# Late convolution taps of a hybrid diffusion step: squares in buffers of their own, one PSUM bank per late accumulator and mean, some taps of chunk 0 as diagonal matrix products

## The chip, the cores and the metric

The kernel runs on one core of a Trainium2 chip. The core has a matrix engine (TensorE, PE in the profile), three engines for element-wise work (VectorE or DVE, ScalarE or ACT, GpSimd or POOL) and a queue that issues the DMAs (SyncE, SP). Each engine executes its own list of instructions in order and waits on semaphores for the others. The metric is the device time of one execution in microseconds, lower is better.

## The reference, cut to what matters

The whole reference is one step of a two-layer backbone on 1024 noisy tokens and 128 context tokens, width 1024, all in float32. Layer 0 mixes with a Conformer convolution, layer 1 with attention, and each layer ends with a convolutional FFN. The change lies in the Conformer convolution of layer 0:

```
def dwconv(x, w, b):                      # depthwise, 31 taps, SAME, per channel
    C = x.shape[-1]
    y = lax.conv_general_dilated(x, w[:, None, :].astype(x.dtype), window_strides=(1,), padding='SAME',
                                 dimension_numbers=('NWC', 'WIO', 'NWC'), feature_group_count=C)
    return y + b

def conformer_conv(h, w_pw1, dw_w, dw_b, ln_g, ln_b, w_pw2):
    a, g = jnp.split(h @ w_pw1, 2, axis=-1)
    u = a * jax.nn.sigmoid(g)
    u = dwconv(u, dw_w, dw_b)
    u = jax.nn.silu(layernorm(u, ln_g, ln_b))
    return u @ w_pw2
...
        x = x + g1 * y                    # y: the mixer's output, g1 from silu(cond) @ ada_w + ada_b
        h = modulate(rmsnorm(x, norm2_g[i]), sh2, sc2)
        x = x + g2 * conv_ffn(h, ffn_w_up[i], ffn_conv_w[i], ffn_conv_b[i], ffn_w_down[i])
```

The layer norm is over all 1024 channels of a token.

## The kernel before, in words

Channels lie on the 128 partitions, in eight blocks j = 0 to 7 (KT = 8); the 1152 tokens lie in the free dimension, in three chunks c of 384 (CH, NCH). Each float32 product is made of three products of split operands (`mm3`, lines 245 to 249: high by high, high by low, low by high); small sums such as the mean are plain float32 products.

The convolution stage runs so. `gated` (line 582) makes u for a block j and a chunk c from two projections. For j = 0 to 5 (WHOLE = 6) the 31 taps run over the whole row of 1167 columns: POOL's share (`taps_pool`, line 645) is a multiplication on ACT into a tile of tag `tmp` (two buffers) and an addition on POOL into `pacc`; DVE's share (`taps_vector`, line 656) is a multiply-add into `da`, a PSUM tile of three banks (tag `acc`); `join` (line 666) adds both into U. For j = 6 and 7 the taps are done later and chunk by chunk in `late_taps(c)` (line 699), 15 taps on POOL (POOL_TAPS_LATE) and 16 on DVE. Its accumulators are the first two banks of one three-bank PSUM tile, `late` (line 696), and the mean of the layer norm is written to the third (line 710).

The loop at lines 761 to 769 then does for each chunk: some steps of `later`, `late_taps(c)`, `layer_norm(c)` at high priority, the reload of the residual stream X[c] from DRAM (`reload`, line 386), and `project_residual` (line 747), the projection with w_pw2 (tiles `pw2p`), eight products of 24 matmuls with the residual addition (L384) and the square sum for the next norm (`add_stat`, line 310: a square on ACT, an addition on POOL, L316 and L317). `norm_mod` of the chunk for the FFN is put into `bg` and moves on at the `tick`s of the next projection; in the last one's case in the FFN.

`layer_norm` (line 709): mean by eight float32 products with a constant matrix (L712), subtraction on DVE (L717), squares on ACT (L724), sums of squares on DVE for blocks 0 to 3 and on POOL for 4 to 7 (L727, L730), two small products (`token_rstd`, `spread`), multiplication on DVE (L736), SiLU on ACT (L740), and the split into ln_h on ACT (L743) and ln_l on DVE (L744). The squares take tiles of tag `tmp`, and so do those of `add_stat` in this projection (the last argument of line 768).

`later` (line 580) are the products of the conditioning vector with ada_w (`ada`, line 252; tile `adaw`, three buffers of 512 KB here, loaded by SP), cut into steps; LATER = (8, 0, 6) of them stand ahead of the three chunks, others in `gated` and `project_residual`. The weights of the projections come through a ring of three raw buffers (`w_raw`), each split by ACT (L220) and DVE (L221).

The order of the instructions on SP is that of the program. On the other engines a planner orders them at build time: an instruction goes where its operands are expected, by the planner's costs, to be ready, in order of priority, which is the order of the program save under `tc.high_priority()`. Buffers of a tag are handed out in the order of the program; a new tile waits until the tile that had the buffer has been read for the last time.

The PSUM has eight banks. In this stage `pool.open` gives four to tag `mm`, three to `acc`, one to `ms` (line 482); `norm_mod` and `ada` take `ms`.

Of the kernel before, what the change touches and what calls it, by code (L numbers as in the profile page):

```python
# [8 lines left out]
F32 = mybir.dt.float32  # L9
F32R = mybir.dt.float32r  # L10
AF = mybir.ActivationFunctionType
ALU = mybir.AluOpType
AX = mybir.AxisListType
PSUM = bass.MemoryType.PSUM
DRAM = bass.MemoryType.DRAM

P = 128
D = 1024
KT = D // P
# [3 lines left out]
CH = 384  # L23
# [7 lines left out]
TAPS = 31  # L31
# [6 lines left out]
RING = 3  # L38
SPLITS = 1
PROMPT_LAG = 2  # L40
POOL_TAPS_LATE = 15
WHOLE = 6
LATER = (8, 0, 6)
NORM_POOL = (1, 3, 5, 7)
# [19 lines left out]
def raw32(t):  # L64
    return t.bitcast(F32)
# [14 lines left out]
def tile_hybrid_step(ctx: ExitStack, tc: tile.TileContext, a: dict, outs: list):  # L80
    nc = tc.nc
# [4 lines left out]
    hp = ctx.enter_context(tc.tile_pool(name="hp", bufs=NCH))  # L86
# [25 lines left out]
    def ntile(name, n=CH, dt=F32):  # L112
        return np_.tile([P, n], dt, tag="n", name=name)
# [7 lines left out]
    def htiles(name):  # L121
        hh = hp.tile([P, KT, CH], F32R, tag="hh", name=f"{name}_h")
        hl = hp.tile([P, KT, CH], F32R, tag="hl", name=f"{name}_l")
        return hh, hl

    class Banks:


        stack = None

        def open(self, **slots):
            if self.stack:
                self.stack.close()
            self.stack = ExitStack()
            self.slots = {
                tag: (self.stack.enter_context(tc.tile_pool(name=f"p_{tag}", bufs=b, space=PSUM, reuse_waits="tile")), n)
                for tag, (b, n) in slots.items()
            }

        def __call__(self, tag, name):  # L140
            pool_, n = self.slots[tag]
# [2 lines left out]
    pool = Banks()  # L144
# [13 lines left out]
    ident = cp.tile([P, P], F32, name="ident")  # L158
# [320 lines left out]
            yield from g  # L479


    pool.open(mm=(4, 512), acc=(1, 1536), ms=(1, 512))


    vec_rows = [
# [24 lines left out]
    slot = lambda tag, *args, **kw: (slot_0 if tag in ("adaw", "vrow") else slot_a)(tag, *args, **kw)  # L510
# [22 lines left out]
    X = [xtile(f"x0_{c}") for c in range(NCH)]  # L533
    acc = acc_tile("acc0")
# [44 lines left out]
    us = []  # L579
    later = chain(*(ada(pool, l, g) for l, g in ((0, 1), (0, 2), (1, 0), (1, 1), (1, 2))))  # L580
# [56 lines left out]
    slot = lambda tag, *args, **kw: (slot_a if tag == "u" else slot_c)(tag, *args, **kw)  # L637

    U = [xtile(f"u_{c}") for c in range(NCH)]
    SPAN = [(0, CH), (CH, 2 * CH), (2 * CH, CONV_N)]  # L640

    def tap(j, t):
        return dww[:, j, t : t + 1]
# [12 lines left out]
    def taps_vector(j, u, d, n, s0_, s1_, fresh):  # L656

        for t in range(n):
            src = u[:, s0_ + t : s1_ + t]
            if t == 0 and fresh:  # L660
                nc.vector.tensor_scalar(d, src, tap(j, t), None, ALU.mult)
            else:
                nc.vector.scalar_tensor_tensor(d, src, tap(j, t), d, ALU.mult, ALU.add)
            yield
# [10 lines left out]
    for j in range(KT):  # L675
# [8 lines left out]
        u = us[j][2]  # L684
        da = pool("acc", f"da{j}")
        pacc = slot("pacc", f"pacc{j}")
        t0 = TAPS - POOL_TAPS
# [5 lines left out]

    L = [None] * NCH
    half = KT // 2
    late = pool("acc", "late").rearrange("p (b n) -> p b n", n=512)
    paccs = {j: slot("pacc", f"pacc{j}") for j in range(WHOLE, KT)}

    def late_taps(c):
        s0_, s1_ = SPAN[c]  # L700
        t0 = TAPS - POOL_TAPS_LATE
        for j in range(WHOLE, KT):
            u, d = us[j][2], late[:, j - WHOLE, 0 : s1_ - s0_]
            taps_pool(j, u, paccs[j], t0, s0_, s1_)
            for _ in taps_vector(j, u, d, t0, s0_, s1_, True):
                pass
            join(j, d, paccs[j], c, s0_)

    def layer_norm(c):
        mu = late[:, KT - WHOLE, 0:CH]  # L710
        for j in range(KT):
            nc.tensor.matmul(mu, mean_w, U[c][:, j, :], start=(j == 0), stop=(j == KT - 1))  # L712
        hh, hl = htiles(f"ln{c}")
        ss = [None, None]
        for g in range(2):
            jj = slice(g * half, (g + 1) * half)
            nc.vector.tensor_tensor(  # L717
                U[c][:, jj, :], U[c][:, jj, :], mu.unsqueeze(1).to_broadcast([P, half, CH]), ALU.subtract
            )
            eng = (nc.vector, nc.gpsimd)[g]  # L720
            for i in range(half // 2):
                sq = slot("tmp", f"lnsq{c}_{g}_{i}")[:, 0 : 2 * CH]
                j0 = g * half + 2 * i
                nc.scalar.activation(sq.rearrange("p (j t) -> p j t", t=CH), U[c][:, j0 : j0 + 2, :], AF.Square)  # L724
                if i == 0:
                    ss[g] = ntile(f"lnss{c}_{g}")
                    eng.tensor_tensor(ss[g], sq[:, 0:CH], sq[:, CH:], ALU.add)  # L727
                else:
                    for o in (0, CH):
                        eng.tensor_tensor(ss[g], ss[g], sq[:, o : o + CH], ALU.add)  # L730
        bank = pool("mm", f"lnv{c}")
        rs = token_rstd(pool, ss, f"lnv{c}", bank)
        pb = spread(pool, rs, f"lnv{c}", bank)
        for g in range(2):
            jj = slice(g * half, (g + 1) * half)
            nc.vector.tensor_tensor(  # L736
                U[c][:, jj, :], U[c][:, jj, :], pb.unsqueeze(1).to_broadcast([P, half, CH]), ALU.mult
            )
            for j in range(g * half, (g + 1) * half):
                nc.scalar.activation(  # L740
                    U[c][:, j, :], U[c][:, j, :], AF.Silu, scale=col("conv_ln_g", j), bias=col("conv_ln_b", j)
                )
            nc.scalar.activation(hh[:, jj, :], U[c][:, jj, :], AF.Copy)  # L743
            nc.vector.tensor_tensor(hl[:, jj, :], U[c][:, jj, :], raw32(hh)[:, jj, :], ALU.subtract)  # L744
        L[c] = (hh, hl)

    def project_residual(H, X, c, acc, l, name, tag):
        for m in range(KT):
            w = weights.take()
            ps = project(pool, w, H[c], f"{name}p{c}_{m}")  # L750
            with tc.high_priority():
                residual(ps, X, m, c, l, 2)
                add_stat(acc, m, c, X[c][:, m, :], tag=tag)
            tick()
            if l == 0 and m % 2:
                next(later, None)

    X = [None] * NCH
    H = [None] * NCH
    acc1 = acc_tile("acc1")  # L760
    for c in range(NCH):
        for _ in range(LATER[c]):
            next(later, None)
        late_taps(c)
        with tc.high_priority():
            layer_norm(c)
        X[c] = reload(0, c, "x1_")
        project_residual(L, X, c, acc1, 0, "pw2", "tmp")
        bg.append(norm_mod(pool, X, acc1, c, 0, 1, H, "n1"))

    for _ in later:
        pass
    pool.open(mm=(5, 512), t=(2, 512), ms=(1, 512))
    sC.close()
    sA.close()
    sF, slot = phase(s=(6, NT), g=(4, NT + 3))
# [13 lines left out]
    sK, slot = phase(s=(4 * NKV, SLOT))  # L790
# [128 lines left out]
    for b in QKV_ORDER:  # L919
        ws = [weights.take(), weights.take()]  # L920
        for tt in range(NTT):
            c, t = divmod(tt, CH // P)
            if H[c] is None:
                drain()
            hh, hl = H[c]
# [187 lines left out]
    for s in range(-3, len(steps)):  # L1113
# [4 lines left out]
        if s >= 0:  # L1118
            i, t = steps[s]
# [24 lines left out]
        if s >= 0:  # L1144
            probs.pop(s)
            i, t = steps[s]
# [13 lines left out]
    sF, slot = phase(s=(6, NT), g=(4, NT + 3))  # L1160
    X = [None] * NCH
# [93 lines left out]
```

## Time and profile before

| | us |
|---|---|
| time of the kernel, median of 3 runs (lowest, highest) | 2887.58 (2884.42, 2888.75) |
| the profiled execution | 2887.7 |
| its span, first to last instruction | 2885.8 |
| PE busy | 2692.8 (93%) |
| DVE busy | 1608.9 (56%) |
| ACT busy | 1083.1 (38%) |
| POOL busy | 758.8 (26%) |
| mean granted TensorE clock, share of full | 0.965 |

Busy shares are means over stages with different limits. The page shows PE's busy share in 40 slices of 72 us: the fifth to the eighth (289 to 577 us), which hold the late taps, layer norms and two of the projections, read 4 5 6 4 tenths, where nearly all later slices read 9. In the rows below, a time at the head of a row is in us from the span's start, `x` counts instructions, and square brackets hold the idle time ahead of an instruction and what ended it.

### The profile page before, as it was taken

What the parts mean: (1) busy time and instruction counts of PE and PEld (TensorE: products, weight loads), DVE (VectorE), ACT (ScalarE), POOL (GpSimd) and SP (SyncE); (2) the same over time, 40 slices, a digit from 0 to 9 for tenths busy, and PEclk for the clock granted to TensorE, in tenths of its full rate; (3) what the DMA queues carried; (4) which work ended last, traced back from release to release, by engine and by line L of the source; (5) the groups of instructions that cost most, each with busy time, mean ns of one, the idle gap of its engine ahead of it and who ended that gap; (6) DMA issues with size and microseconds to landing.
All of it is one profiled execution on the core that took longest, in us unless ns stands there. A gap on an engine that the chain in (4) does not pass through costs nothing.

```text
span 2885.8 us, 40019 instructions
## 1 busy us (share of the span) xinstructions
PE 2692.8 (93%) x15863; PEld 2568.6 (89%) x15863; DVE 1608.9 (56%) x2793; ACT 1083.1 (38%) x2110; POOL 758.8 (26%) x840
## 2 busy tenths in 40 slices
PE   7999456499999999999999899999999999999999
PEld 4888155299999999999999889989999999999998
DVE  6899746355444444445464578876544444444445
ACT  5555444342222222221365677765421222122222
POOL 3799643520000000000256556644200000000003
PEclk9999677799999999999999999999999999999999
DMA  7554233331111111111120000025211111111111
GB/s 252 181 156 146 95 110 103 94 104 43 44 45 44 44 45 44 38 43 37 64 93 29 1 1 1 1 79 163 73 37 44 45 44 37 44 44 32 43 52 66
DMA packets 194419, 192.18 MB, mean 67 GB/s; under 512 B 7072, under 2 KB 173323, under 8 KB 192698
## 3 DMA queue, kind: packets, MB, share of 16 engines
q1 hardware_dynamic: 193946, 189.53, 21.0%
q8 instruction: 125, 2.05, 0.3%
q14 instruction: 60, 0.49, 0.1%
q0 software_dynamic: 288, 0.11, 0.0%
HBM read 175.19 MB, written 14.42 MB: 66 GB/s over the span
## 4 chain that ended last, share of the span: by engine, by line
PE 87%; DVE 6%; POOL 3%; DMA 2%; ACT 2%; issue 1%; SPq 0%; DVEq 0%; POOLq 0%; ACTq 0%
PE f1pd L247 3%; PE f1pd L249 3%; PE f1pd L248 3%; PE f1pg L249 3%; PE f0pg L249 3%; PE f1pg L248 3%; PE f0pg L248 3%; PE f0pv L247 3%; PE f1pv L247 3%; PE f0pg L247 3%; PE f1pg L247 3%; PE f1pv L248 3%; PE f0pv L248 3%; PE f0pv L249 3%; PE f1pv L249 3%; PE f0pd L247 3%
## 5 line engine op out<-in xcount | busy, mean ns | idle before, releaser
L220 ACT ACTIVATE w_hi<-w_raw 128x1024 fp32r<-128x1024 f32 x208 | 218.1, 1058 | 923.2 <-PE f0pd L248 223.7
L221 DVE TENSOR_TENSOR w_lo<-w_raw,w_hi 128x1024 fp32r<-128x1024 f32 x208 | 280.6, 1358 | 425.9 <-ACT w_hi L220 425.7
L654 POOL TENSOR_TENSOR pacc<-pacc,tmp 128x1167 f32<-128x1167 f32 (+2 forms) x156 | 291.4, 1870 | 36.1 <-ACT tmp L653 13.5
L384 DVE SCALAR_TENSOR_TENSOR x<-f1pd,mods,x 128x256 f32<-128x256 f32 (+1 forms) x352 | 170.2, 514 | 102.7 <-PE f1pd L249 102.4
L384 DVE SCALAR_TENSOR_TENSOR x<-f0pd,mods,x 128x256 f32<-128x256 f32 (+1 forms) x352 | 169.8, 514 | 99.1 <-PE f0pd L249 98.9
L411 POOL MEMSET f1gp<- 128x1 f32 x66 | 3.6, 99 | 703.8 <-DVE f1gp L435 690.8
L411 POOL MEMSET f0gp<- 128x1 f32 x66 | 3.6, 99 | 703.8 <-DVE f0gp L435 690.8
L1063 POOL TENSOR_TENSOR pr<-pr,sm 128x384 f32<-128x384 f32 x192 | 154.0, 831 | 107.4 <-DVE sm L1061 53.8
L653 ACT ACTIVATE tmp<-u,dww 128x1167 f32<-128x1167 f32 (+2 forms) x156 | 142.6, 918 | 97.0 <-POOL pacc L654 94.6
L248 PE MATMUL f1pd<-f1al,w_hi 128*128 128x384 f32 x528 | 178.6, 338 | 0.0
L249 PE MATMUL f1pd<-f1ah,w_lo 128*128 128x384 f32 x528 | 178.5, 338 | 0.0
L249 PE MATMUL f0pd<-f0ah,w_lo 128*128 128x384 f32 x528 | 178.5, 338 | 0.0
L248 PE MATMUL f0pd<-f0al,w_hi 128*128 128x384 f32 x528 | 178.4, 338 | 0.0
L247 PE MATMUL f1pd<-f1ah,w_hi 128*128 128x384 f32 x528 | 178.4, 339 | 0.0
L247 PE MATMUL f0pd<-f0ah,w_hi 128*128 128x384 f32 x528 | 177.8, 338 | 0.0
L249 PE MATMUL f0pg<-n_h,w_lo 128*128 128x384 f32 x528 | 176.5, 334 | 0.0
L249 PE MATMUL f1pg<-n_h,w_lo 128*128 128x384 f32 x528 | 176.5, 334 | 0.0
L248 PE MATMUL f0pg<-n_l,w_hi 128*128 128x384 f32 x528 | 176.5, 334 | 0.0
L248 PE MATMUL f1pg<-n_l,w_hi 128*128 128x384 f32 x528 | 176.5, 334 | 0.0
L247 PE MATMUL f0pg<-n_h,w_hi 128*128 128x384 f32 x528 | 176.4, 334 | 0.0
L247 PE MATMUL f1pg<-n_h,w_hi 128*128 128x384 f32 x528 | 176.4, 334 | 0.0
L248 PE MATMUL f0pv<-n_l,w_hi 128*128 128x384 f32 x528 | 176.4, 334 | 0.0
(323 smaller groups left out, 7829.5 us busy)
## 6 DMA issues: line engine op xcount, KB each, us to landing
adaw<-in_ada_w_dram SPq DMA_DIRECT2D x96, 512.0 KB, 5.0
w_raw<-in_ffn_w_up_dram SPq DMA_DIRECT2D x88, 512.0 KB, 3.8
w_raw<-in_ffn_w_down_dram SPq DMA_DIRECT2D x44, 512.0 KB, 3.7
w_raw<-in_conv_w_pw_dram SPq DMA_DIRECT2D x40, 512.0 KB, 7.0
w_raw<-in_attn_w_o_dram SPq DMA_DIRECT2D x24, 512.0 KB, 4.3
xs_d<-x SPq DMA_DIRECT2D x6, 1536.0 KB, 11.5
x<-xs_d SPq DMA_DIRECT2D x6, 1536.0 KB, 7.0
w_raw<-in_attn_w_qkv_dram SPq DMA_DIRECT2D x12, 512.0 KB, 3.7
```

The costliest lines, as they stand in the source:

```text
L220: nc.scalar.activation(hi, raw, AF.Copy)
L221: nc.vector.tensor_tensor(lo, raw, raw32(hi), ALU.subtract)
L247: nc.tensor.matmul(ps, wh, mh, start=first, stop=False)
L248: nc.tensor.matmul(ps, wh, ml, start=False, stop=False)
L249: nc.tensor.matmul(ps, wl, mh, start=False, stop=last)
L384: nc.vector.scalar_tensor_tensor(xx, ps[:, lo:hi], mod(l, v, j, cond), xx, ALU.mult, ALU.add)
L411: nc.gpsimd.memset(gp[:, z : z + 1], 0.0)
L653: nc.scalar.activation(tmp, u[:, s0_ + t : s1_ + t], AF.Copy, scale=tap(j, t))
L654: nc.gpsimd.tensor_tensor(d, d, tmp, ALU.add)
L1063: nc.gpsimd.tensor_tensor(pr[n], pr[n], ri.to_broadcast([P, CH]), ALU.mult)
```

## The change

The late taps get a table LATE_TAPS with two numbers a chunk: how many taps are products on PE, and how many are POOL's. Chunk 0 has 12 on PE, 7 on POOL and 12 on DVE; chunks 1 and 2 have none on PE, 12 on POOL and 19 on DVE. A tap on PE is a float32 product of u with a 128x128 diagonal matrix that ACT makes from the identity and the tap's column; twelve of them accumulate in the bank to which DVE adds its taps. The matrices lie in a tile of tag `hh`. The steps of `later` that stood ahead of a chunk's taps stand behind these products now.

The three-bank tag `acc` is closed after the whole blocks and replaced by `la`, three tiles of one bank: each late accumulator and each mean is a tile of its own. The squares of the layer norm lie in one tile of tag `hl`, and the sums go into the first square of each half in place of a tile of their own; the squares of `add_stat` in this projection take tiles of the norm pool (`ntile`, six buffers). So `tmp` serves the taps alone.

```
-POOL_TAPS_LATE = 15
+LATE_TAPS = ((12, 7), (0, 12), (0, 12))
...
-    pool.open(mm=(4, 512), acc=(1, 1536), ms=(1, 512))
+    pool.open(mm=(4, 512), ms=(1, 512))
+    sacc = ExitStack()
+    pool.add(sacc, acc=(1, 1536))
...
-    late = pool("acc", "late").rearrange("p (b n) -> p b n", n=512)
+    sacc.close()
+    pool.add(sacc, la=(3, 512))
...
     def late_taps(c):
         s0_, s1_ = SPAN[c]
-        t0 = TAPS - POOL_TAPS_LATE
-        for j in range(WHOLE, KT):
-            u, d = us[j][2], late[:, j - WHOLE, 0 : s1_ - s0_]
+        n, t0 = LATE_TAPS[c]
+        t0 = TAPS - t0
+        te = t0 - n
+        ds = {j: pool("la", f"late{j}_{c}")[:, 0 : s1_ - s0_] for j in range(WHOLE, KT)}
+        if n:
+            diag = hp.tile([P, (KT - WHOLE) * n, P], F32, tag="hh", name=f"diag{c}")
+            for i, (j, t) in enumerate((j, t) for j in ds for t in range(te, t0)):
+                nc.scalar.activation(diag[:, i, :], ident, AF.Copy, scale=tap(j, t))
+                nc.tensor.matmul(
+                    ds[j], diag[:, i, :], us[j][2][:, s0_ + t : s1_ + t], start=(t == te), stop=(t == t0 - 1)
+                )
+        for _ in range(LATER[c]):
+            next(later, None)
+        for j, d in ds.items():
+            u = us[j][2]
             taps_pool(j, u, paccs[j], t0, s0_, s1_)
-            for _ in taps_vector(j, u, d, t0, s0_, s1_, True):
+            for _ in taps_vector(j, u, d, te, s0_, s1_, not n):
                 pass
             join(j, d, paccs[j], c, s0_)
     def layer_norm(c):
-        mu = late[:, KT - WHOLE, 0:CH]
+        mu = pool("la", f"mu{c}")[:, 0:CH]
...
+        sq = hp.tile([P, KT, CH], F32, tag="hl", name=f"lnsq{c}")
...
-                sq = slot("tmp", f"lnsq{c}_{g}_{i}")[:, 0 : 2 * CH]
                 j0 = g * half + 2 * i
-                nc.scalar.activation(sq.rearrange("p (j t) -> p j t", t=CH), U[c][:, j0 : j0 + 2, :], AF.Square)
...
+                nc.scalar.activation(sq[:, j0 : j0 + 2, :], U[c][:, j0 : j0 + 2, :], AF.Square)
+                ss[g] = sq[:, g * half]
+                for j in range(j0, j0 + 2):
+                    if j > g * half:
+                        eng.tensor_tensor(ss[g], ss[g], sq[:, j], ALU.add)
...
     for c in range(NCH):
-        for _ in range(LATER[c]):
-            next(later, None)
         late_taps(c)
...
-        project_residual(L, X, c, acc1, 0, "pw2", "tmp")
+        project_residual(L, X, c, acc1, 0, "pw2", None)
...
+    sacc.close()
     pool.open(mm=(5, 512), t=(2, 512), ms=(1, 512))
```

`pool.add` is the loop that opens PSUM tags, taken out of `Banks.open` so that a tag can be closed by itself.

## Rows read from the trace of the kernel before

**Rows 1.** Busy us by stretch: PE, PEld, DVE, ACT, POOL; PE clock, DMA share, GB/s.
```profile
311.00:371.00 60.00, 21.17 (x61) 9.89 (x57) 40.92 (x60) 28.54 (x42) 27.72 (x28) 0.61 0.11 36
371.00:411.00 40.00, 37.20 (x205) 34.70 (x205) 16.77 (x18) 13.11 (x18) 9.86 (x7) 0.95 0.67 197
411.00:478.00 67.00, 19.72 (x63) 15.00 (x64) 38.48 (x56) 32.01 (x51) 34.00 (x35) 0.57 0.00 0
478.00:514.00 36.00, 35.67 (x209) 31.21 (x207) 16.09 (x20) 13.95 (x20) 13.54 (x11) 1.00 0.88 263
514.00:587.00 73.00, 31.07 (x99) 17.06 (x100) 29.55 (x43) 32.92 (x53) 35.89 (x35) 0.65 0.20 65
587.00:622.00 35.00, 33.86 (x196) 33.18 (x195) 18.27 (x30) 13.33 (x19) 14.08 (x11) 1.00 0.67 196
```
**Rows 2.** Waits of PE, 311 to 622: us in total, times, longest.
```profile
PE late L712 <- DVE u L669: 62.3, 3, 29.6
PE pw2p L247 <- ACT ln_h L743: 21.9, 3, 8.1
```

**Rows 3.** Timeline of POOL, tap additions of the three chunks: start, us.
```profile
314.27 24.53 POOL L654 TENSOR_TENSOR pacc<-pacc,tmp 128x384 f32<-128x384 f32 x23 [0.72 <-ACT tmp L653]
...
411.52 29.86 POOL L654 TENSOR_TENSOR pacc<-pacc,tmp 128x384 f32<-128x384 f32 x28
...
515.07 15.43 POOL L654 TENSOR_TENSOR pacc<-pacc,tmp 128x399 f32<-128x399 f32 x14
```

**Rows 4.** Timeline of ACT, squares of the first layer norm.
```profile
349.15 1.58 ACT L724 ACTIVATE lnsq<-u 128x768 f32<-128x768 f32 x2 [11.85 <-DVE u L717]
...
353.17 0.84 ACT L724 ACTIVATE lnsq<-u 128x768 f32<-128x768 f32 x1 [1.10 <-POOL lnss L727]
```

**Rows 5.** Timeline of DVE, late taps and joins, and the next norm.
```profile
311.86 9.84 DVE L663 SCALAR_TENSOR_TENSOR late<-u,dww,late 128x384 f32<-128x384 f32 x15
323.92 0.56 DVE L669 TENSOR_TENSOR u<-late,pacc 128x384 f32<-128x384 f32 x1 [2.23 <-POOL pacc L654]
324.51 0.62 DVE L661 TENSOR_SCALAR late<-u,dww 128x384 f32<-128x384 f32 x1
...
353.48 5.22 DVE L663 SCALAR_TENSOR_TENSOR late<-u,dww,late 128x384 f32<-128x384 f32 x8
...
426.50 0.56 DVE L669 TENSOR_TENSOR u<-late,pacc 128x384 f32<-128x384 f32 x1 [15.79 <-POOL pacc L654]
427.09 0.62 DVE L661 TENSOR_SCALAR late<-u,dww 128x384 f32<-128x384 f32 x1
...
467.94 3.23 DVE L356 SCALAR_TENSOR_TENSOR n_u<-x,gsc,n_b 128x384 f32<-128x384 f32 x6
```

**Rows 6.** Busy us of L712 (PE, PEld) by stretch, PE clock, DMA share, GB/s.
```profile
339.40:344.10 4.70, 4.65 (x8) 2.53 (x9) 0.50 0.01 3
344.10:347.30 3.20, 3.17 (x10) 1.62 (x8) 0.97 0.00 0
```

**Rows 7.** Timeline of PE, ada products beside the late taps of chunk 0.
```profile
313.33 4.40 PE L270 MATMUL ada<-adaw,cs 128*32 128x512 f32 x12 [1.34 <-DMA adaw<-in_ada_w_dram]
```

**Rows 8.** Chain of work in time, mean of chunk 0 and start of its projection.
```profile
339.45 7.83 PE late L712 x16
...
371.34 0.69 PE pw2p L248
```

**Rows 9.** Groups by line and shape: busy us, mean ns of one, idle before.
```profile
L859 ACT ACTIVATE qk_1xn<-pqkv,qk_r 128x128 f32<-128x128 f32 x10 | 3.1, 365 | 1.7 <-POOL qk_r L334 1.7
```

**Rows 10.** Timeline of DVE, two weight splits.
```profile
262.70 3.71 DVE L221 TENSOR_TENSOR w_lo<-w_raw,w_hi 128x1024 fp32r<-128x1024 f32 x1
...
388.56 1.22 DVE L221 TENSOR_TENSOR w_lo<-w_raw,w_hi 128x1024 fp32r<-128x1024 f32 x1 [2.46 <-ACT w_hi L220]
```

**Rows 11.** Groups by line and shape on DVE, 311 to 622.
```profile
L744 DVE TENSOR_TENSOR ln_l<-u,ln_h 128x1536 fp32r<-128x1536 f32 x6 | 10.5, 1756 | 5.4 <-ACT ln_h L743 5.4
```

**Rows 12.** Timeline of SP, the ada loads ahead of chunk 2.
```profile
505.10 24.25 SPq L258 DMA_DIRECT2D adaw<-in_ada_w_dram  x10
```

More of the change, by code (lines that the diff above doesn't have):

```diff
@@ L134, in open, with add @@
             self.stack = ExitStack()
[L135 to L138, printed above, removed]
+            self.slots = {}
+            self.add(self.stack, **slots)
+        def add(self, stack, **slots):
+            for tag, (b, n) in slots.items():
+                pool_ = tc.tile_pool(name=f"p_{tag}", bufs=b, space=PSUM, reuse_waits="tile")
+                self.slots[tag] = (stack.enter_context(pool_), n)
         def __call__(self, tag, name):
@@ L721, in layer_norm @@
             for i in range(half // 2):
-                sq = slot("tmp", f"lnsq{c}_{g}_{i}")[:, 0 : 2 * CH]
                 j0 = g * half + 2 * i
-                nc.scalar.activation(sq.rearrange("p (j t) -> p j t", t=CH), U[c][:, j0 : j0 + 2, :], AF.Square)
[L725 to L730, printed above, removed]
+                nc.scalar.activation(sq[:, j0 : j0 + 2, :], U[c][:, j0 : j0 + 2, :], AF.Square)
[3 more added lines that the diff above has]
+                        eng.tensor_tensor(ss[g], ss[g], sq[:, j], ALU.add)
         bank = pool("mm", f"lnv{c}")
```

## The prediction

> **What bounds the kernel now.** I read the busy time by stage first [rows 1]. Three chunks of 384 tokens pass one after the other through an approach (late taps, then the layer norm) and a projection (pw2p). The approaches take 60, 67 and 73 us, with TensorE (PE) busy 21, 20 and 31 us of them at a mean granted clock of 0.57 to 0.65; the projections take 40, 36 and 35 us with PE nearly full. The reader is to see that the approach of a chunk begins only where the projection before it ends: 200 us of approach in a row, between stages that PE fills.
>
> Then PE's waits in that stretch [rows 2]: 62.3 us for the join of the late taps (L669) and 21.9 us for ln_h, the end of the layer norm. So the path runs through taps, join, mean, layer norm, projection, three times.
>
> Then who makes the join late. On POOL [rows 3] the 28 tap additions of chunk 1 run in one piece from 411.52, and chunk 2's from 515.07; in chunk 0's projection POOL is busy 9.9 of 40 us [rows 1]. It could have begun earlier: u and pacc are long there. What holds it is the two tmp buffers. The squares of the layer norm and those of the projection take them as well, in the order of the program, so a tap of chunk 1 gets one only after chunk 0's last square. The squares themselves show it: two leave at 349.15, the fourth at 353.17 waits for a POOL addition to give its buffer back [rows 4]. DVE has the other half of it [rows 5]: j=6 of chunk 1 ran inside the layer norm of chunk 0 (eight taps from 353.48), but the first tap of j=7 stands at 427.09, directly behind the join of j=6 at 426.50, and in chunk 0 likewise (324.51 behind 323.92, although DVE had idled 2.23 us). All late accumulators and the mean are one PSUM tile.
>
> **The change, part by part.** The sum is made against the profiled execution: 2887.7 us, of which the span is 2885.8 and 1.9 lies around it; the median of the runs is 2887.58, the same for this purpose.
>
> *Diagonal products.* For j=6 and j=7 of chunk 0, PE takes 12 taps each: 24 products with a 128x128 fp32 weight over 384 columns. That is the shape of the mean product L712, of which the trace has two passes a product, 16 in all: seven filled 4.65 us at clock 0.50 (the eighth only touches that window), nine 3.17 us at 0.97 [rows 6], 0.66 and 0.35 us a pass. So a product costs 1.33 us at half clock and 0.70 at full, 24 cost between 17 and 32 us. L712 itself ran its first seven passes at half clock, so I take four products at half clock and twenty at full, 19.3 us. They can't start before the accumulator of j=5, whose banks they take, is joined: 311.2, where the first late tap stands now (0.66 before the second at 311.86 [rows 5]). PE also holds the ada products, which wait for their loads at that time (12 in 4.40 us behind a wait of 1.34 [rows 7]); I add 1 us to either twelve. Then j=6's products end at 323 (311.2 + 4 x 1.33 + 8 x 0.70 + 1) and j=7's at 332.5. DVE adds its 12 taps behind each: 12 x 0.656 us (the fifteen of a row in 9.84 [rows 5]) = 7.9, a join 0.6: j=6 joined at 331.5, j=7 at 341. Before, the mean began at 339.45 [rows 8]. This part costs 1.5 us: DVE idles 12 us for the products and saves 8 taps, 5.2 us. Bounds: -3 (all at full clock, no ada in the way) to +19 us (all at half clock, then 12 taps and the join, with 8 us of ada ahead of them). Building 24 diagonals is ACT work on 128x128 with a scale per partition; the nearest row takes 0.365 us [rows 9], so 9 us. They lie between 272 and 311, where ACT only feeds POOL; without that cover they would be late by 9 us, which is inside the bound.
>
> *POOL and ACT.* POOL's additions fall from 28 a chunk to 12, 22 and 22. At 1.07 us (23 in 24.53 [rows 3]) and 1.10 for chunk 2 (14 in 15.43), with 4 of chunk 0's before 311 (28 less the 23 and one shortly ahead), the last of chunk 0 is done at about 321, of chunk 1 at 345, of chunk 2 at 369 plus 4 for the layer norm. Nothing else asks for tmp now. So POOL leaves the path altogether: it is done with the last chunk when the first projection begins. The squares leave in one piece (4 x 0.84 us), which takes 1.4 us from each layer norm. Against that, POOL's additions now run under DVE's work. DVE's w_lo, with both inputs in SBUF, took 3.71 us where POOL ran long tap additions and 1.22 where it was idle [rows 10], while taps, with one input in PSUM, keep 0.656 beside them. Five instructions of the first layer norm have both inputs in SBUF (three sums of squares, two of L744); with at most one 1.0 us addition in front of each they cost up to 5 us; I take 1.4, so that the first layer norm keeps its length.
>
> The Trainium skill, page "SBUF — State Buffer", section "Who interferes with whom", says that a VectorE instruction with two SBUF inputs contends with a GpSimd instruction that reads SBUF, and that the one that comes second waits for the whole of the other. The w_lo pair agrees. It speaks against moving additions under the layer norm; by it the first projection would begin up to 5 us later, less the 1.4 already counted, and the sum end near 2795.
>
> *A bank for each accumulator and mean.* Three banks go round: j=6, j=7, mean. Chunk 1's j=6 may start when chunk 0's j=6 is joined, j=7 when j=7 is, without a wait for the mean or the other join. DVE's taps are now 12, 19, 19 in place of 16 for each j.
>
> *DVE, which becomes the engine to count.* From 341: the mean takes 7.83 us, the rest of the layer norm to the projection 24.1 (371.34 - 347.3) [rows 8]. In these DVE had room for 11 taps (7.8/0.656, idle before) and 16 (as before). Of chunk 1's 38 taps 11 are left when the projection begins at 373 (341 + 31.9; 371.3 before). There DVE is busy 16.8 of 40 us [rows 1]; 11 taps (7.2) and the joins (1.1) take 8.3/0.58 = 14 us: chunk 1 joined at 387. Its mean now meets a PE at full clock: 16 x 0.35 = 5.6, then 24.1: layer norm 1 ready at 417. PE has 40 + 5.6 + 2.4 (mean and small products) of work from 373: the projection ends at 421. So projection 1 starts at 421 in place of 478: 57 us won.
>
> Chunk 2, 38 taps of 399 columns at 0.656 x 399/384 = 0.68: 25.9 us. From 387 to 421 DVE's 34 us go to the projection (11), to layer norm 1 (six of 1.756 as L744 [rows 11], three sums of 0.55: 12.2) and leave 11 us, 16 taps. Left: 22 taps 15.0, joins 1.2, and the norm of chunk 0 for the next stage, which comes first in the program (six of its eight L356 take 3.23 [rows 5], with four L364, taken alike, 6.4): 22.6 us at the 55% that projection 1 leaves (16.1 of 36 busy [rows 1]): 41 us, joined at 462. Mean 5.6, layer norm 24.1: projection 2 at 492, in place of 587: 95 us won. Projection 1 is done on PE at 465 (36 and 8 more), so some 27 us of PE's idleness stay.
>
> *Cover.* The loads: SP issues the ada loads of this stage over 24.25 us from 505.10 [rows 12], 27 us behind the start of projection 1; moved with it they end at 472, before the reload of chunk 2 is free to go at 492. Where that cover is gone each us of lateness goes into projection 2 after four of its products. The squares of add_stat now take buffers of the norm pool; POOL's additions empty them in time, as they did with two.
>
> **Sum.** 2887.7 - 95 = 2793 us. What follows is the same work, held by PE.
>
> **Rivals.**
> (a) Only one chunk hides. DVE is in-order, and if joins and taps of chunk 2 fall behind projection 1 and the norm of chunk 0, chunk 2 stays serial: 57 won, 2831 us. For it: DVE's count above leaves it no slack. Against: the planner did put 16 taps into the gaps of a layer norm [rows 5].
> (b) The change doesn't do what it says: chunk 1's taps still wait for the projection, because another shared thing (ACT's order, the mm banks) holds them. Then only the shorter POOL chains count: chunk 1 goes from 29.9 to 25 us (DVE's 38 taps), chunk 2 by about 8 less, squares 4: 2887.7 - 17 = 2871 us. Against: what stands in front of the additions in [rows 3, 4] is tmp, and the change takes that away.
> (c) Slower, by the diagonal products: PE sits cold behind the ada loads, all 24 cost 1.33 us, and the join of chunk 0 comes 19 us late. It decides if the last of them ends later than 332.5; each us after that is a us on the path. With the taps of the other chunks held as in (b), and half of its 17 us, 2887.7 + 19 - 9 = 2898 us. For it: clock 0.61 in that stretch [rows 1]. Against: it needs the taps of the other chunks to stay in order as well.
>
> **How the numbers follow.** Forecast 0.60, (a) 0.26, (b) 0.08, (c) 0.06. The forecast's own spread is 2768 (projection 0 five us sooner, and chunk 2's taps ahead of the norm, which takes 6.4/0.55 = 12 from its wait, and 8 for a DVE that in all this isn't held up: 120 won) to 2812; (a) spreads to about 2850. Range 2768 to 2845. A measurement tells 0.2%, 5.8 us, from no change. Faster 0.93 (the first two and most of (b)), the same 0.02, slower 0.05.
>
> **What would show it.** POOL's chunk-1 additions start near 321 and not at 411; the first tap of j=7 of chunk 1 stands before the join of its j=6; the mean of chunk 1 lies inside the first projection; PE's wait for L669 falls from 62 to some 35 us; the next stage starts near 527 in place of 622. Wrong: POOL's additions still behind the projection's squares (b), the mean of chunk 0 later than 345 (c), or DVE idle while chunk 2's taps are outstanding (a).

## The result: 2812 us, 0.974 of the kernel before

The changed kernel takes 2812.12 us (median of 4 runs, 2810.35 to 2812.89) against 2888.16 us of the kernel before in runs beside it: a ratio of 0.9738, 95% interval 0.9721 to 0.9755, some 76 us. The profiled execution has a span of 2810.8 us (2885.8 before), mean granted clock 0.981 (0.965).

All of it is won before the FFN. Its first product starts at 544.20 us, before the change at 619.53: 75.3 us earlier, as much as the medians differ by. So the start of the FFN serves below as a second measure beside the ratio. From there to the end the traces below take between 2262.6 and 2268.7 us, so it is good to some 3 us.

The changed kernel by stretch (columns as in [rows 1]; the stretches are the approach of chunk 0, projection 0, the gap behind it, projection 1, the gap behind that, projection 2):

```profile
308.00:382.00 74.00, 39.99 (x127) 20.08 (x125) 55.12 (x92) 42.89 (x68) 55.85 (x55) 0.75 0.14 43
382.00:428.00 46.00, 46.00 (x244) 41.06 (x244) 37.97 (x51) 17.82 (x24) 19.56 (x13) 0.94 0.58 172
428.00:436.40 8.40, 2.73 (x16) 2.16 (x14) 4.89 (x6) 7.28 (x12) 1.86 (x2) 0.72 0.00 0
436.40:488.50 52.10, 46.29 (x230) 41.44 (x230) 27.16 (x34) 20.89 (x32) 17.45 (x14) 0.85 0.61 182
488.50:500.70 12.20, 8.24 (x30) 1.15 (x29) 8.50 (x6) 8.57 (x12) 0.99 (x1) 0.72 0.65 202
500.70:544.20 43.50, 41.82 (x230) 35.82 (x229) 23.70 (x38) 16.77 (x27) 15.42 (x14) 1.00 0.65 196
```

Of the three approaches of 60, 67 and 73 us [rows 1] one is left. Those of chunks 1 and 2 lie inside the stretches before them, and what remains of them are gaps of 8.4 and 12.2 us. The first approach has become longer: projection 0 starts at 381.9, before the change at 369.5.

TensorE's waits from 308 to 545 us (total, times, longest), to be read against [rows 2]:

```profile
PE ada L274 <- DMA adaw<-in_ada_w_dram: 13.0, 7, 3.6
PE pw2p L251 <- ACT ln_h L761: 11.7, 2, 10.8
PE mu L732 <- DVE u L675: 7.7, 1, 7.7
PE mu L732 <- DVE u L738: 4.4, 1, 4.4
PE lnv L346 <- POOL lnv_r L338: 4.2, 1, 4.2
```

The join, 62.3 us in three waits, costs 7.7 us in one. POOL's timeline says why (start, us), against [rows 3]:

```profile
310.61 38.38 POOL L660 TENSOR_TENSOR pacc<-pacc,tmp 128x384 f32<-128x384 f32 x36 [1.53 <-ACT tmp L659]
357.03 1.03 POOL L660 TENSOR_TENSOR pacc<-pacc,tmp 128x399 f32<-128x399 f32 x1 [8.05 <-ACT tmp L659]
...
382.50 5.91 POOL L660 TENSOR_TENSOR pacc<-pacc,tmp 128x399 f32<-128x399 f32 x3 [0.86 <-ACT tmp L659]
```

The 36 additions in one piece, whose row shows only the shape of the first, are the last nine of chunk 0, all 22 of chunk 1 (320.1 to 343.6) and the first five of chunk 2; chunk 1's began at 411.52 before. Chunk 2's are done at 388.4 instead of 551.

DVE's late taps and joins (start, us), against [rows 5]:

```profile
325.72 7.87 DVE L669 SCALAR_TENSOR_TENSOR late<-u,dww,late 128x384 f32<-128x384 f32 x12 [17.71 <-PE late L717]
333.69 0.56 DVE L675 TENSOR_TENSOR u<-late,pacc 128x384 f32<-128x384 f32 x1
...
337.33 12.70 DVE L669 SCALAR_TENSOR_TENSOR late<-u,dww,late 128x384 f32<-128x384 f32 x24 [0.46 <-PE late L717]
349.94 0.55 DVE L675 TENSOR_TENSOR u<-late,pacc 128x384 f32<-128x384 f32 x1
...
417.07 0.62 DVE L675 TENSOR_TENSOR u<-late,pacc 128x256 f32<-128x256 f32 x2
```

DVE stood idle for 17.71 us, waiting for the diagonal products of j=6. Behind them the 12 taps of j=7 of chunk 0 and 12 of chunk 1's j=6 take turns (x24). The last join of chunk 2 ends at 417.7.

On TensorE the products came late, since ada products that waited for their loads stood before them:

```profile
311.04 1.05 PE L274 MATMUL ada<-adaw,cs 128*32 128x512 f32 x4 [1.56 <-DMA adaw<-in_ada_w_dram]
315.04 1.42 PE L274 MATMUL ada<-adaw,cs 128*32 128x512 f32 x4 [2.95 <-DMA adaw<-in_ada_w_dram]
316.39 9.93 PE L717 MATMUL late<-u,diag 128*128 128x384 f32 x26
326.16 4.03 PE L732 MATMUL mu<-u,mean_w 128*128 128x384 f32 x12
330.03 7.26 PE L717 MATMUL late<-u,diag 128*128 128x384 f32 x22
```

### The profile page after: what moved, and what is told of

The parts are those of the page before. It is cut to its first block, busy times and chain, and to the rows that moved or that the text cites. A ratio compares the mean times of both kernels' runs of the same rounds, so it can differ in the third digit from the quotient of the medians.

```text
span 2810.8 us, 40051 instructions
## 1 busy us (share of the span) xinstructions
PE 2697.4 (96%) x15911; PEld 2571.0 (91%) x15911; DVE 1606.2 (57%) x2797; ACT 1070.9 (38%) x2106; POOL 733.5 (26%) x812
## 4 chain that ended last, share of the span: by engine, by line
PE 89%; DVE 5%; DMA 3%; ACT 2%; POOL 1%; issue 1%; SPq 0%; DVEq 0%; POOLq 0%; ACTq 0%
PE f1pd L253 3%; PE f1pd L251 3%; PE f1pd L252 3%; PE f0pg L253 3%; PE f1pg L252 3%; PE f1pg L253 3%; PE f0pg L251 3%; PE f0pv L253 3%; PE f1pg L251 3%; PE f1pv L252 3%; PE f1pv L251 3%; PE f0pg L252 3%; PE f0pv L251 3%; PE f0pv L252 3%; PE f1pv L253 3%; PE f0pd L252 3%
## 5 line engine op out<-in xcount | busy, mean ns | idle before, releaser
L660 POOL TENSOR_TENSOR pacc<-pacc,tmp 128x1167 f32<-128x1167 f32 (+2 forms) x128 | 265.9, 2081 | 41.3 <-ACT tmp L659 33.9
L252 PE MATMUL f1pd<-f1al,w_hi 128*128 128x384 f32 x528 | 178.6, 338 | 0.0
L252 PE MATMUL f0pd<-f0al,w_hi 128*128 128x384 f32 x528 | 178.4, 338 | 0.0
L252 PE MATMUL f0pg<-n_l,w_hi 128*128 128x384 f32 x528 | 176.5, 334 | 0.0
L252 PE MATMUL f1pg<-n_l,w_hi 128*128 128x384 f32 x528 | 176.5, 334 | 0.0
L252 PE MATMUL f0pv<-n_l,w_hi 128*128 128x384 f32 x528 | 176.4, 334 | 0.0
L252 PE MATMUL f1pv<-n_l,w_hi 128*128 128x384 f32 x528 | 176.4, 334 | 0.0
```

Of the source, the lines that this page charges most:

```text
L252: nc.tensor.matmul(ps, wh, ml, start=False, stop=False)
L660: nc.gpsimd.tensor_tensor(d, d, tmp, ALU.add)
```

## The experiments

Each run was timed beside the kernel before; the ratio stands with its 95% interval, and differences in us are ratios times 2888. "FFN" is the start of the FFN's first product in the trace (619.5 before, 544.2 changed).

**One tile again (the banks undone).**

```diff
-    pool.add(sacc, la=(3, 512))
+    pool.add(sacc, la=(1, 1536))
+    late = pool("la", "late").rearrange("p (b n) -> p b n", n=512)
...
-        mu = pool("la", f"mu{c}")[:, 0:CH]
+        mu = late[:, KT - WHOLE, 0:CH]
```

> The changed kernel with its banks undone: the late accumulators and the mean are again three banks of one tile; squares and diagonals stay as changed. Theory: VectorE's first taps of chunk 1 then wait for the last read of the mean of chunk 0 (the subtraction, 353 us) and those of chunk 2 for that of chunk 1, so taps and joins of the next chunk again stand behind the layer norm and the projections: 20 to 50 us of the 76 come back, 2832 to 2862. Rival: the squares alone carried the gain, and the time stays within 8 us of 2812.

Ratio 0.9770 (0.9755 to 0.9785), 2818.94 us; FFN 552.8. The rival's bound holds for the time: the banks are worth 7 us by the medians and 9 by the ratios. The order of which the theory spoke is seen nevertheless. DVE (start, us):

```profile
343.05 7.87 DVE L669 SCALAR_TENSOR_TENSOR late<-u,dww,late 128x384 f32<-128x384 f32 x12
351.02 0.56 DVE L675 TENSOR_TENSOR u<-late,pacc 128x384 f32<-128x384 f32 x1
360.12 3.42 DVE L739 TENSOR_TENSOR u<-u,late 128x1536 f32<-128x1536 f32 x2 [8.55 <-PE late L733]
...
363.93 0.61 DVE L667 TENSOR_SCALAR late<-u,dww 128x384 f32<-128x384 f32 x1
```

No tap of chunk 1 runs before the subtraction of chunk 0's mean (360.12) has read it. But these taps then fit into the layer norm and projection 0, inside which chunk 1 is joined (401.9, against 381.8 in the changed kernel). What the one tile is seen to cost lies ahead of projection 0, on TensorE:

```profile
351.63 8.46 PE L733 MATMUL late<-u,mean_w 128*128 128x384 f32 x16 [11.36 <-DVE u L675]
```

All 16 passes of the mean of chunk 0 run behind the last join. In the changed kernel, where the mean has a bank of its own, 12 of them had run at 326.16, and the mean was complete at 352.2 instead of 360.1. Projection 0 starts 5.3 us later (387.2).

**Both kinds of squares back in tmp.** The layer norm's four squares use `slot("tmp", ...)` with sums of their own again, and the statistics of the projections too:

```diff
-        project_residual(L, X, c, acc1, 0, "pw2", None)
+        project_residual(L, X, c, acc1, 0, "pw2", "tmp")
```

> The changed kernel with its squares undone: those of the layer norm and of the projections' statistics share the two tmp buffers with the taps again; banks and diagonals stay as changed. Theory: GpSimd's taps of chunks 1 and 2 then stand behind the squares of the layer norm and of the projection before, as they did before the change: 40 to 75 us of the 76 come back, 2852 to 2887. Rival: the banks alone carried the gain, and the time stays within 8 us of 2812.

Ratio 0.9946 (0.9931 to 0.9961), 2869.63 us; FFN 601.1. Some 60 of the 76 us come back: the squares carry the gain.

**Only the statistics' squares back in tmp** (the line above alone).

> The changed kernel with only the squares of the projections' statistics back in the two tmp buffers; those of the layer norm stay apart. Theory: this is the tie that counted: in the tmp buffers the taps of chunk 1 stand behind the squares of the eight blocks of projection 0, so they end with that projection, and 40 to 57 of the 57.5 us that undoing both cost come here: 2852 to 2870. Rival: the layer norm's squares are the tie; then this costs less than 15 us, up to 2827.

Ratio 0.9943 (0.9926 to 0.9960), 2870.90 us; FFN 604.9: as much as both. ACT's timeline (start, us) shows the tie itself:

```profile
413.63 0.50 ACT L320 ACTIVATE sq<-x 128x384 f32<-128x384 f32 x1
...
417.78 0.51 ACT L320 ACTIVATE sq<-x 128x384 f32<-128x384 f32 x1
418.19 0.60 ACT L659 ACTIVATE tmp<-u,dww 128x384 f32<-128x384 f32 x1
420.01 0.61 ACT L659 ACTIVATE tmp<-u,dww 128x384 f32<-128x384 f32 x1 [1.22 <-POOL acc L321]
```

The first tap of chunk 1 (L659) leaves directly behind the square of projection 0's last block (417.78), the second when POOL has added that square (L321) and so given its buffer back.

**Only the layer norm's squares back in tmp.**

> The changed kernel with only the layer norm's squares back in the two tmp buffers (with their own sums, as in the kernel before); those of the projections' statistics stay apart. Theory: in the tmp buffers the taps of chunk 1 then stand behind the four squares of the layer norm of chunk 0, which are done at about 360 us, when chunk 1 still has slack: 5 to 25 us are lost, 2817 to 2837. Rival: the layer norm's squares are the tie and this costs 40 us or more, 2852 and up.

Ratio 0.9818 (0.9804 to 0.9833), 2832.87 us; FFN 566.6. POOL's additions of chunk 1 run from 361.36 instead of directly behind chunk 0's, 23 us are lost, within what the theory gave. The two costs (23 and 59) don't add up to that of both (60): a chunk held by the statistics is held later than by the layer norm.

**The diagonals alone.** One tile and both kinds of squares undone, the diagonals kept.

> The diagonal products alone: squares in the tmp buffers and the late accumulators and mean in one tile, as in the kernel before; chunk 0 has 12 diagonal products, 7 taps on GpSimd and 12 on VectorE for each late tile. Theory: the diagonals win nothing for chunk 0 (projection 0 started at 375.9 us with them when the squares were undone, at 369.5 in the kernel before) and nothing frees chunks 1 and 2: 2880 to 2897. Rival: with the squares undone the changed kernel still won 15.5 us (2869.6 against 2885.1), and it was the diagonals that won them, not the banks: 2865 to 2875.

Ratio 1.0013 (1.0003 to 1.0022), 2889.01 us; FFN 619.4 (before 619.5). Nothing is won: projection 0 starts at 380.4 against 369.5 before, and what is lost there does not reach the FFN.

**No diagonals.**

```diff
-LATE_TAPS = ((12, 7), (0, 12), (0, 12))
+LATE_TAPS = ((0, 12), (0, 12), (0, 12))
```

> The changed kernel without the diagonal products: chunk 0's late tiles take 12 taps on GpSimd and 19 on VectorE, as chunks 1 and 2 do. Theory: the diagonals don't pay, because they stand behind ada loads on TensorE (first at 316.39 us, last at 337.33) while VectorE is free from 308.0; 38 taps of 0.42 us or less take 14 to 16 us, so both joins of chunk 0 are done by about 327 to 335 instead of 349.9, projection 0 starts at about 365 to 370 instead of 381.9, and the FFN starts 5 to 12 us before 544.2: some 2800 to 2807. Rival: the diagonals save the time that they were built for, VectorE has the taps of chunk 1 behind those 38, and the kernel gets 5 to 15 us slower (2817 to 2827).

Ratio 0.9695 (0.9681 to 0.9710), 2797.24 us; FFN 529.7, 14.5 us earlier than with them. DVE (start, us):

```profile
310.93 1.14 DVE L667 TENSOR_SCALAR late<-u,dww 128x384 f32<-128x384 f32 x2
311.98 18.99 DVE L669 SCALAR_TENSOR_TENSOR late<-u,dww,late 128x384 f32<-128x384 f32 x36
330.88 0.55 DVE L675 TENSOR_TENSOR u<-late,pacc 128x384 f32<-128x384 f32 x1
...
332.14 0.56 DVE L675 TENSOR_TENSOR u<-late,pacc 128x384 f32<-128x384 f32 x1
...
335.23 3.41 DVE L738 TENSOR_TENSOR u<-u,mu 128x1536 f32<-128x1536 f32 x2
```

All 38 taps of chunk 0 are done at 331.0, before DVE ended even those of j=6 with the diagonals (333.6), and the subtraction of the mean stands at 335.23 instead of 353.02. Projection 0 starts at 364.0, 17.9 us earlier. The gain is larger than the theory gave, though its 0.42 us a tap is shown by no run: the 38 took 20.0 us, 0.53 us each.

**The squares alone** (one tile and no diagonals).

> The squares alone: of the change only the squares in buffers of their own stay; the late accumulators and the mean are one tile of three banks again, and chunk 0 has no diagonals (12 taps on GpSimd, 19 on VectorE). Theory: the three parts nearly add up, squares carrying most; undoing the banks cost 6.8 us and leaving out the diagonals gave 14.9, so 2812.1 + 6.8 - 14.9 = 2804, within 2797 to 2811. Rival: the banks matter more once VectorE has 38 taps instead of 24 for chunk 0, since those of chunk 1 then wait for the mean behind them: 2815 or more.

Ratio 0.9721 (0.9705 to 0.9737), 2806.18 us; FFN 539.1 (the sum of the parts, 544.2 + 8.6 - 14.5, is 538.3). One of the three edits is worth as much as the whole change; the intervals overlap. Against the kernel without diagonals it is again the mean of chunk 0 that comes later, 344.3 against 334.4, and with it projection 0 (373.0 against 364.0). The new split of the taps of chunks 1 and 2 (12 on POOL, 19 on DVE) is in this run as in all others; what it is worth by itself was not tried, so the squares are shown to carry the gain together with it.

**No ada steps in the last gate.** In the gate of j = 7 the two `next(later, None)` are left out, and `LATER` is (8, 0, 10).

> The changed kernel, diagonals kept, but the four ada steps of the last gate (j = 7) are moved behind the taps of chunk 2. Theory: the diagonal products were late because TensorE worked through ada products that waited for their loads (3.05, 1.56, 2.95 us) ahead of the first of them at 316.39; without those the first comes at about 309 to 311, both joins of chunk 0 are done by about 343 instead of 349.9, projection 0 starts at about 375 instead of 381.9, and 3 to 7 us come off 2812. Rival: the diagonals themselves and VectorE's two tap chains in turn set the joins; projection 0 starts within 2 us of 381.9 and the time is not below 2809.

Ratio 0.9771 (0.9757 to 0.9784), 2819.78 us. TensorE (start, us):

```profile
309.74 1.05 PE L274 MATMUL ada<-adaw,cs 128*32 128x512 f32 x4 [0.27 <-DMA adaw<-in_ada_w_dram]
310.72 8.65 PE L717 MATMUL late<-u,diag 128*128 128x384 f32 x26
```

The place was right and the time was not. The products begin at 310.72 instead of 316.39, the last join of chunk 0 ends at 343.5 instead of 350.5, projection 0 at 374.9, seven us earlier as expected. But the four steps have to be done before the FFN all the same, and from projection 0 to the FFN it now takes 174.5 us instead of 162.3: it starts at 549.4.

**The layer norm's small products in the mean's bank.**

```diff
-        mu = pool("la", f"mu{c}")[:, 0:CH]
+        bank = pool("la", f"mu{c}")
+        mu = bank[:, 0:CH]
...
-        bank = pool("mm", f"lnv{c}")
```

> The changed kernel with one edit: the small products of the layer norm (sums and spread) go into the mean's own bank instead of a tile of the tag mm. Theory: in the changed kernel these products of chunks 1 and 2 wait for the mm bank that projection 0 (projection 1) releases only with its last blocks: lnv1 ran at 422.06 us and lnv2 at 479.40 us, right behind the first product of the last block (421.89, 478.92), though the sums of chunk 1 were done at about 395. With the edit lnv1 runs at about 396 to 400, the last low half of chunk 1 is written by about 415 instead of 436, projection 1 follows projection 0 with no hole at 428 to 437 (4.0 us of TensorE work in 10 us there), and the FFN starts at about 532 instead of 544.2: 10 to 15 us faster, some 2800. Rival: the order of TensorE's own queue holds the small products back, not the bank; then lnv1 stays within 3 us of 422 and the time within 5 us of 2812.

In the changed kernel, on TensorE (start, us):

```profile
421.89 0.33 PE L251 MATMUL pw2p<-ln_h,w_hi 128*128 128x384 f32 x1
422.06 1.39 PE L329 MATMUL lnv<-ones,lnsq 128*128 128x1 f32 x12
...
427.40 0.83 PE L346 MATMUL lnv<-ident,lnv_r 128*128 128x128 f32 x6
...
436.37 1.01 PE L251 MATMUL pw2p<-ln_h,w_hi 128*128 128x384 f32 x2 [0.84 <-ACT ln_h L761]
```

With the edit:

```profile
394.56 1.39 PE L329 MATMUL mu<-ones,lnsq 128*128 128x1 f32 x12
402.00 0.94 PE L346 MATMUL mu<-ident,lnv_r 128*128 128x128 f32 x6
```

Ratio 0.9719 (0.9703 to 0.9735), 2804.78 us; FFN 537.9, 6.3 us earlier. The sums come 27.5 us sooner and projection 1 follows projection 0 without a hole at 430.5. So it was the bank that held them: a tile of the tag mm, asked for in the program behind the eight blocks of the projection, and filled only inside the last of them. At 422.06 TensorE waits for nothing; it is their place in its list that the choice of the bank had set. The gain is half of what the theory gave: projection 2, which begins at 480.6 (500.75 in the changed kernel), runs into the ada products and their loads. SP issues the reload of chunk 2 behind ten of these loads, at 500.20, and the first residual addition of chunk 2 runs at 509.39; the stretch up to the FFN takes 57 us instead of 43.5.

**Both of these** (no diagonals, the mean's bank).

> Both edits at once: no diagonal products, and the layer norm's small products in the mean's bank. Without the diagonals (2797 us) TensorE still stood nearly idle from 409.4 to 422.5 us, between projections 0 and 1, because the small products of chunk 1 ran at 402.5 to 412.8 behind projection 0. Theory (each edit takes away a wait of its own): these 13 us go, projection 1 follows projection 0 at about 410, and 7 to 13 us come off the 2797: 2784 to 2790. Rival (one sum is limited further down, by the transfers of projections 1 and 2 in SyncE's queue): the time stays within 4 us of 2797.

Ratio 0.9670 (0.9657 to 0.9684), 2792.09 us; FFN 523.3, 6.4 us below the kernel without diagonals and 14.6 below the one with the bank: the two edits add up. By the medians the second one brings 5.2 us, between the theory's 7 and the rival's 4. The hole of 13 us is gone (projection 1 starts at 411.8), but what the rival named is there as well: SP issues the reload of chunk 2 behind ten ada loads at 486.70, 20 us after projection 2 began (467.0). By stretch, approach of chunk 0 and the rest up to the FFN:

```profile
308.00:364.60 56.60, 25.65 (x77) 11.79 (x73) 54.21 (x95) 36.20 (x58) 44.47 (x45) 0.65 0.16 51
364.60:523.30 158.70, 143.48 (x743) 119.01 (x744) 113.03 (x148) 81.64 (x123) 77.18 (x63) 0.92 0.59 180
```

From projection 0 on, TensorE is busy 143.5 of 158.7 us. What is left is the approach of chunk 0, in which DVE has work for 54.2 of 56.6 us.

**More ada steps in the gates.** On the kernel with both edits:

```diff
         if j:
             next(later, None)
+            if c == 0:
+                next(later, None)
```

> The kernel with both edits, and seven more steps of the ada products issued in the gate stage (two in place of one at chunk 0 of each gate), so that fewer are left for projections 1 and 2. Theory: in these two projections TensorE waits for ada loads (16 us in the changed kernel, 16.3 without diagonals, from 295 to 545 us), since an ada load in SyncE's queue stands behind a buffer and holds the loads behind it; the gate stage has transfers to spare, so half of these waits go and the time is 5 to 10 us below the kernel with both edits. Rival: the gate stage ends later by what is taken out, or waits for its own loads, and the time is the same within 3 us or longer.

Ratio 0.9670 (0.9657 to 0.9684), 2791.53 us: no difference; FFN 527.7 (of the two profiled executions this one is 3 us the longer). From projection 0 to the FFN it takes 149.8 us instead of 158.7, but projection 0 starts at 377.9 instead of 364.6. The rival holds, as it did in the run without ada steps in the last gate: what one stretch gains by moving these products, the other loses.

**Ten taps on POOL for chunk 0.** On the same kernel, `LATE_TAPS = ((0, 10), (0, 12), (0, 12))`.

> The kernel with both edits, with 10 instead of 12 taps of chunk 0 on GpSimd (21 on VectorE). Theory: GpSimd's 24 additions of 1.07 us from 310.6 end at about 336 and so set the second join of chunk 0, which VectorE could have had 3 to 4 us earlier; with 20 additions the last pass of the mean comes about 3 us earlier and the time falls by 1 to 4 us. Rival: VectorE's chain of dependent taps sets the join, and the time is the same or up to 3 us longer.

Ratio 0.9661 (0.9648 to 0.9674), 2788.25 us, the fastest median here, but not told apart from 2792.09. The theory's mechanism is not there: the last join came at 335.1, later than with twelve (332.3), so DVE's chain sets it, as the rival said. This version and the two with both edits beat the kernel before and the changed one.

## Why the prediction was right, and where its steps were not

The time, forecast at 2793, came out 19 us longer, inside its range and at the upper end of the forecast's own spread (2812), by the mechanism that it gave first. The FFN starts at 544.2 (some 527 forecast), PE waits 7.7 us for the joins (35 forecast). Two chunks hide, not one (rival a), and tmp was the tie: chunk 1's taps no longer stand behind the projection (rival b is out), and both are shown by the run with the statistics' squares undone. The first tap of j=7 of chunk 1 runs at 350.92, before the join of its j=6 at 356.87, as forecast; of the mean of chunk 1 only the last product lies inside projection 0 (383.02), seven ran before it (356.57). Rival (c)'s signs are there: the last diagonal product ended at 337.3, after 332.5, and the mean of chunk 0 was complete at 352.2, after 345 (the forecast's own working, 341 and 7.8 us, already has it at 348.8). But the other chunks were free, so it never made the kernel slower.

- *POOL.* Additions of chunk 1 were put at 321 to 345 and ran from 320.1 to 343.6. Right. Chunk 2's ended at 388.4 instead of 369 (373 with the layer norm's); its taps on DVE lasted until 417, so nothing waited for them.
- *A bank for each.* The waits that [rows 5] show for taps of one tile were read rightly, but given half of the credit. The banks bring 7 to 9 us; what was won rests on the squares. And what the banks are seen to bring was not counted: the prediction let the whole mean of chunk 0 follow the last join (7.83 us), where only 1.65 us of it did (350.54).
- *Diagonals.* 24 products took 9.93 + 7.26 = 17.2 us (19.3 forecast), and j=6 was joined at 334.2 (331.5 forecast). Their start failed: 316.39, not 311.2, and 12 of 17.7 us of DVE's idleness were foreseen. j=7 was joined at 350.5 instead of 341: its products ended at 337.3, 4.8 us after the 332.5 of the forecast, and chunk 1's taps took turns with its own. Against that, six of the eight mean products had run at 326, and the mean was complete at 352.2 instead of 348.8. The whole part was priced against the old split of the taps, at 1.5 us. Against the new split without diagonals, which was not worked out, it costs 14.5 us.
- *Layer norm 0.* "Keeps its length", 24.1 us from the end of the mean to the first product with a low half (L252), was wrong: it takes 31.5 (352.2 to 383.7). DVE, POOL and ACT hold other chunks' taps in front of it, as these rows of DVE show:

```profile
361.74 1.27 DVE L748 TENSOR_TENSOR lnsq<-lnsq 128x384 f32<-128x384 f32 x1
362.94 5.42 DVE L669 SCALAR_TENSOR_TENSOR late<-u,dww,late 128x384 f32<-128x384 f32 x10
368.26 0.15 DVE L336 TENSOR_SCALAR lnv_m<-lnv 128x3 f32<-128x3 f32 x1
```

  The sums were on hand at 365.2; the tiny L336 stood behind ten taps, of chunks 1 and 2 in turn, until 368.26. On ACT the table for the SiLU, 1.28 us, is loaded at 373.25 behind a tap, where before the change it was loaded at 354.03 while ACT had nothing else to do. The contention that was priced at 1.4 us is also there: the three sums of squares take 1.14, 1.28 and 1.27 us beside POOL's additions, and end 0.41 to 0.42 us behind those (358.06, 360.33, 362.60); two of the three in the kernel without diagonals take 0.56 and 0.55, so it costs 2.0 us. By the Trainium skill, page "SBUF — State Buffer", section "Who interferes with whom", a VectorE instruction with two SBUF inputs contends with a GpSimd instruction that reads SBUF, and the one that comes second waits for the whole of the other; the rows agree. The two L762, 1.76 and 1.75 us, cost nothing more than before [rows 11]; there it is three of POOL's additions that take 5.91 us (the row at 382.50 above).
- *Projection 0* thus had its first product with a low half at 383.7, not 373: 3.4 us are the mean, 7.4 the layer norm.
- *Projection 1* was put at 421 and started at 436.4. Chunk 1 was joined at 381.8 (387 forecast), so DVE was quicker than counted. The failed term is the 24.1 us from mean to projection, which took no account of the bank of the tag mm: the sums of squares were ready at 395, and their products ran at 422.06.
- *Projection 2* was put at 492 and started at 500.75. Two mistakes stand against each other here, and that the start is only some 10 us off is luck. DVE's count was too slow, the join at 417.7 instead of 462; but the squares of the layer norm then waited for 35 us in ACT's queue:

```profile
456.89 0.60 ACT L367 ACTIVATE n_h<-n_u,mods 128x384 fp32r<-128x384 f32 x1
457.90 0.60 ACT L367 ACTIVATE n_h<-n_u,mods 128x384 fp32r<-128x384 f32 x1
458.41 3.04 ACT L744 ACTIVATE lnsq<-u 128x768 f32<-128x768 f32 x4
```

  The norm of chunk 0 for the next stage comes first in the program, which the prediction counted for DVE and not for ACT; weight splits and squares of projection 1 stand there too. Behind it the small products again waited for mm, until 479.40 (457.0 in the run with the mean's bank).
- *Cover.* The ada loads were to end at 472. SP (start, us), against [rows 12]:

```profile
464.69 7.37 SPq L262 DMA_DIRECT2D adaw<-in_ada_w_dram  x2
...
480.62 27.09 SPq L262 DMA_DIRECT2D adaw<-in_ada_w_dram  x10
507.77 1.21 SPq L392 DMA_DIRECT2D x<-xs_d  x1
```

  They moved by 24 us, not by 57, and the reload of chunk 2 left behind them at 507.77, seven us after its projection had begun. In the runs with the mean's bank, with and without diagonals, projection 2 starts earlier, the reload leaves 20 us behind its start, and it takes 57 and 56 us. The two runs that moved ada steps gave nothing or lost; the reload ahead of these ten loads was not tried.

The sum also counts its gain from the stretches of [rows 1], which begin where a projection is dense. Before the change the first product of projection 2 with a low half ran at 582.76, not at 587; by the same working 91 us are won, not 95, and the forecast would be 2797.

The diagonals and the bank together cost as much as is missing against the forecast: the kernel without both is 19.6 us below the changed one by the ratios (0.9738 less 0.9670, times 2888). That the two figures meet is partly luck, since the forecast had the diagonals in it, counted DVE's work too long and did not see what held chunk 2. So the mechanism was right, and the closeness of the time owes something to errors that cancel. Why the planner put ACT's squares of chunk 2 behind the norm of chunk 0 was not tried, and stays open.

## What to carry to other kernels

Where a stage starts late, look for the buffer ring that it shares with a stage before it, and ask who took the last turn: two scratch buffers shared by taps and statistics cost 59 us here, with no engine full. After such a tie is cut, look at once for the next ring that runs through the same stages in the order of the program (here the mm banks). And price a part of a change against the change without it, not only against the kernel before.

## What the runs showed of the hardware

A DVE tap that adds to its predecessor's result costs 0.656 us, one whose predecessor worked on another accumulator 0.53 us: 12 of one chain in 7.87 us, 24 of two chains in turn in 12.70, and 36 in 18.99 without diagonals. The single records are of nearly the same length (623 and 615 ns). So the records of alternating chains overlap by some 0.09 us, and those of one chain stand 0.03 us apart. The Trainium skill, page "Perfetto Trace Analysis", section "DVE / Act Engine Instruction (TENSOR_ADD, Activation, etc)", has a record end only when the write is acknowledged, and lets the next instruction fetch its data before that; the alternating rows agree. That in one chain the next tap waits for the write would explain its rows, but no run here shows the wait itself. The prediction took 0.656 for every tap, which for the 38 taps of chunk 1, if all of them alternate, is 4.9 us too much.
